# A hybrid decoder layer in split fp32: groups of 3, 4, 4 in the first FFN, earlier weight splits, later low halves, scaling from PSUM

## The chip, the cores and the metric

The kernel runs on one core of a Trainium2 chip. Its engines work from queues of their own, in order: TensorE (PE) multiplies, with its weight loads as PEld; VectorE (DVE), ScalarE (ACT) and GpSimd (POOL) do the elementwise work; DMAs are issued from SyncE (SP), ACT and POOL. The metric is the device time of one execution in microseconds.

## The reference

512 rows of 1024 columns get 16 learned rows ahead of them (528 rows), and pass one layer: half a SwiGLU FFN, a mixer (a gated short convolution beside forgetting attention), half a second FFN, a final norm.

```python
def swiglu_ffn(h, w_gu, w_down):
    gate, up = jnp.split(h @ w_gu, 2, axis=-1)
    return (jax.nn.silu(gate) * up) @ w_down
...
    h = jnp.concatenate([meta, x], axis=1)
    for l in range(DEPTH):
        h = h + 0.5 * swiglu_ffn(rms_norm(h, ffn1_norm[l]), ffn1_w_gu[l], ffn1_w_down[l])
        h = h + hybrid_mixer(rms_norm(h, mix_norm[l]), w_in[l], conv_w[l], b_f[l],
                             out_norm_conv[l], out_norm_attn[l], w_out[l])
        h = h + 0.5 * swiglu_ffn(rms_norm(h, ffn2_norm[l]), ffn2_w_gu[l], ffn2_w_down[l])
    h = h[:, N_META:]
    return rms_norm(h, final_norm)
```

The FFN's inner width is 2816, that is 22 tiles of 128 columns; a pair is two of them.

## The kernel before

Activations lie transposed (`hT`, 8 tiles of 128 rows of the model width by 528 columns). Every fp32 operand is split in a rounded high half, which ACT casts (hi), and a rest, which DVE takes by subtraction (lo). A product is then three matmuls, hi·hi, hi·lo and lo·hi.

Most of an FFN runs in units of a Strassen-like scheme (`products`). A unit takes a block of 256 output columns, cuts the rows in two halves (264 columns each in FFN1, 256 in FFN2) and makes seven products in place of eight, each in a slot of its own: nj pairs of k tiles, 3·nj matmuls. Slot b is the product of the weight form "nat" with B11; slot b + 1 is the last product (p4) of the unit before; then nat·B21, B·T2 with weight "s24", E·T1 with "s1", B·T3 with "s3" and C·B22. The PSUM banks A, B, C and E are reused within a unit: B starts as -A, copied by ACT at b + 1 (L535), and C as -B at b + 4 (L536), the latter beside the E product.

The weight forms come from `prep`: SP loads the raw block 15 slots ahead (L470), ACT copies one quarter (L474), POOL issues two accumulating DMAs (L478), DVE makes two adds (`s2` L481, `s4` L484), then ACT casts each form (L492) and DVE takes the low half (L496). The operand's forms of a pair come from `pair_forms`: sums on POOL (L379 to L382), casts on ACT (L368), low halves on DVE (L369). `x_pair` does so for the input, `hidden_pair` for the result of gate and up.

The first six column tiles of FFN1 and the first ones of FFN2 go the plain way (`classical`, `prep_classical`: load, cast L450, low half L454; 48 matmuls of L318 a tile), so that PE has work while forms are made. Then `gates` and `ups` of two tiles each alternate, with four pairs, and between them the `down` units, four for each group of hidden pairs: 3, 3, 2 and 3 in FFN1, and 3, 3 and 4 in FFN2. As the last group of FFN1 finishes a tile of `hT`, `operand` makes the mixer's operand from it: hi by ACT (L275), lo by DVE (L280), and `squares` adds on POOL (L290).

The order is written by hand: `sl.slot` appends a product, and `sl.at(t, work, prio)` sets the other engines' work at a slot number; each engine takes its work in the order of slots and, within one, of prio. At the end `finish(i)` norms the four row tiles of 128: squares and row sums on ACT, gain on DVE, the norm's few steps on ACT and DVE, scaling by it on ACT (L1230) and DVE (L1232), and one DMA for each half.

## Time and profile before

| | |
|---|---|
| median of three runs | 996.2 us (993.84 to 996.5) |
| profiled execution, its own time | 994.59 us |
| its span, first to last instruction | 992.6 us |
| PE, DVE, ACT, POOL busy | 96%, 79%, 59%, 35% |
| mean granted clock of PE | 0.989 |
| chain that ended last | PE 73%, DVE 15%, ACT 5% |

The span is 2.0 us shorter than the time. The chain's shares say which engine's work stood on the path that ended last, over the whole span; what a stretch is short of must be read from that stretch, from PE's idle time and from the clock that was granted there. A matmul that begins an idle time names in brackets how long PE stood and who ended it.

### The profile page before, as it was taken

Reading aid. Unit: us, or ns where it says so; the run is one execution under the profiler, and the core shown is the slowest. Engines: PE = TensorE matmul, PEld = TensorE weight load, DVE = VectorE, ACT = ScalarE, POOL = GpSimd, SP = SyncE. Lnnn points to the kernel's source line nnn. Section 1 sums busy time; section 2 is a strip of 40 time slices with the busy share of each in tenths; the row PEclk is TensorE's granted clock in tenths of the full one; section 3 lists DMA queues with packets and bytes.
Section 4 is the critical chain, followed back from the end, with each engine's and each line's share of the span. In section 5 each row is a group of like instructions: output and inputs, shape, how many; then the busy total and the mean of one; then the engine's idle time right before and its main releaser. Section 6 shows DMA issues by size and latency. Waiting matters only on the chain.

```text
span 992.6 us, 17859 instructions
## 1 busy us (share of the span) xinstructions
PE 948.9 (96%) x7022; PEld 905.7 (91%) x7022; DVE 780.0 (79%) x1260; ACT 583.3 (59%) x1036; POOL 345.6 (35%) x319
## 2 busy tenths in 40 slices
PE   9898999999999898999999999999999999999994
PEld 8798999999999887989899978778999999999993
DVE  5688887888788887786777666778887888788764
ACT  5545655665576564775656665446555665667444
POOL 4347533543444563100000000266443553354300
PEclk9999999999999999999999999999999999999998
DMA  6237488668784571532222221247778668787712
GB/s 194 65 107 145 118 174 159 148 120 181 171 151 97 117 142 32 144 103 60 74 66 78 57 84 43 64 137 151 138 157 190 132 133 181 146 180 149 174 29 86
DMA packets 173188, 121.01 MB, mean 122 GB/s; under 512 B 5844, under 2 KB 171520, under 8 KB 173104
## 3 DMA queue, kind: packets, MB, share of 16 engines
q1 hardware_dynamic: 113376, 89.37, 29.6%
q0 software_dynamic: 59008, 28.93, 23.9%
q10 hardware_dynamic: 720, 1.57, 0.4%
q8 instruction: 55, 0.90, 0.4%
q14 instruction: 29, 0.24, 0.1%
HBM read 117.69 MB, written 2.10 MB: 121 GB/s over the span
## 4 chain that ended last, share of the span: by engine, by line
PE 73%; DVE 15%; ACT 5%; issue 4%; DMA 1%; POOL 1%; SPq 0%; ACTq 0%; DVEq 0%
PE bank L522 47%; PE bank L318 20%; DVE w_lo L496 4%; DVE arena L369 2%; PE bank L1055 2%; DMA raw<-in_ffn_w_gu_dram 1%; DVE hT L604 1%; PE bank L1210 1%; DVE w_lo L454 1%; PE bank L992 1%; PE bank L1022 1%; ACT arena L275 1%; DVE w_lo L81 1%; DVE xn L398 1%; PE acc L318 1%
## 5 line engine op out<-in xcount | busy, mean ns | idle before, releaser
L522 PE MATMUL bank<-arena,w_hi 128*128 128x256 f32 (+1 forms) x3080 | 567.7, 286 | 13.3 <-ACT bank L536 7.7
L522 PEld LDWEIGHTS bank<-arena,w_hi 128*128 128x128 f32 x3080 | 481.7, 191 | 19.7 <-ACT bank L536 11.4
L522 PE MATMUL bank<-arena,w_lo 128*128 128x264 f32 (+1 forms) x1540 | 439.1, 285 | 4.2 <-DVE w_lo L496 4.2
L522 PEld LDWEIGHTS bank<-arena,w_lo 128*128 128x128 f32 x1540 | 294.6, 191 | 5.5 <-DVE w_lo L496 5.2
L492 ACT CAST w_hi<-raw 128x1024 fp32r<-128x1024 f32 (+2 forms) x186 | 176.3, 948 | 137.1 <-DVE raw L484 109.7
L318 PE MATMUL bank<-arena,w_hi 128*128 128x264 f32 (+2 forms) x1152 | 246.6, 322 | 2.6 <-ACT w_hi L450 2.6
L496 DVE TENSOR_TENSOR w_lo<-raw,w_hi 128x1024 fp32r<-128x1024 f32 (+2 forms) x186 | 222.9, 1199 | 25.8 <-ACT w_hi L492 24.2
L318 PEld LDWEIGHTS bank<-arena,w_hi 128*128 128x128 f32 x1152 | 178.9, 190 | 18.4 <-ACT w_hi L450 3.0
L318 PE MATMUL bank<-arena,w_lo 128*128 128x264 f32 (+2 forms) x576 | 155.0, 323 | 5.3 <-DVE w_lo L454 5.3
L318 PEld LDWEIGHTS bank<-arena,w_lo 128*128 128x128 f32 x576 | 96.2, 190 | 15.8 <-DVE w_lo L454 8.2
L478 POOL DMA_DIRECT2D raw<-in_ffn_w_gu_dram x34 | 44.1, 1297 | 82.2 <-DMA raw<-in_ffn_w_gu_dram 81.2
L478 POOL DMA_DIRECT2D s<-in_ffn_w_gu_dram x34 | 50.6, 1489 | 61.0 <-ACT bank L536 60.2
L80 ACT CAST w_hi<-raw 128x1024 fp32r<-128x1024 f32 (+3 forms) x54 | 44.1, 828 | 45.9 <-PE bank L318 36.0
L81 DVE TENSOR_TENSOR w_lo<-raw,w_hi 128x1024 fp32r<-128x1024 f32 (+2 forms) x53 | 55.3, 1052 | 18.0 <-ACT w_hi L80 17.7
L478 POOL DMA_DIRECT2D s<-in_ffn_w_down_dram x28 | 41.2, 1472 | 69.1 <-ACT bank L536 63.5
L604 DVE TENSOR_TENSOR hT<-bank,hT 128x264 f32<-128x264 f32 (+1 forms) x112 | 47.5, 424 | 14.9 <-PE bank L522 14.1
L496 DVE TENSOR_TENSOR w_lo<-s,w_hi 128x512 fp32r<-128x512 f32 (+2 forms) x62 | 46.8, 755 | 0.0
L193 ACT ACTIVATE s<-s 128x256 f32<-128x256 f32 (+3 forms) x42 | 19.3, 460 | 46.1 <-DVE s L561 26.7
L474 ACT COPY s<-raw 128x512 f32<-128x512 f32 (+2 forms) x62 | 35.5, 572 | 18.5 <-DVE w_lo L496 15.6
L481 DVE TENSOR_TENSOR raw<-raw 128x512 f32<-128x512 f32 (+2 forms) x62 | 41.4, 669 | 0.8
L369 DVE TENSOR_TENSOR arena<-ts,arena 128x1056 fp32r<-128x1056 f32 (+1 forms) x29 | 35.9, 1237 | 7.5 <-ACT arena L368 7.5
L478 POOL DMA_DIRECT2D raw<-in_ffn_w_down_dram x28 | 35.4, 1264 | 15.2 <-DMA raw<-in_ffn_w_down_dram 14.5
(229 smaller groups left out, 1158.0 us busy)
## 6 DMA issues: line engine op xcount, KB each, us to landing
raw<-in_ffn_w_gu_dram SPq DMA_DIRECT2D x34, 1024.0 KB, 7.0
raw<-in_ffn_w_down_dram SPq DMA_DIRECT2D x20, 768.0 KB, 4.4
raw<-in_w_in_dram SPq DMA_DIRECT2D x24, 512.0 KB, 4.0
raw<-in_ffn_w_gu_dram POOLq DMA_DIRECT2D x34, 256.0 KB, 4.7
s<-in_ffn_w_gu_dram POOLq DMA_DIRECT2D x34, 256.0 KB, 6.3
raw<-in_ffn_w_gu_dram SPq DMA_DIRECT2D x16, 512.0 KB, 4.0
raw<-in_ffn_w_down_dram SPq DMA_DIRECT2D x4, 1024.0 KB, 5.1
raw<-in_ffn_w_down_dram POOLq DMA_DIRECT2D x20, 192.0 KB, 4.4
```

The source lines that it names most:

```text
L80: nc.scalar.copy(h, src)
L81: nc.vector.tensor_sub(lw, src, h.bitcast(F32))
L318: nc.tensor.matmul(ap, lhsT=wt[:, kw, :], rhs=mt[:, k, c0 - off:c1 - off], start=(first and a == 0 and b == 0), stop=(last and a == len(ks ...
L369: self.sl.at(t + 1, lambda: nc.vector.tensor_sub(lo, src(), hi.bitcast(F32)), 2)
L474: nc.scalar.copy(raw["s3"], raw["all"][:, 0::2, 0])
L478: nc.gpsimd.dma_start(out=t, in_=mat_j[:, i, :, c0 + P:c0 + 2 * P], accum_op=ALU.add)
L481: nc.vector.tensor_add(raw["all"][:, 0::2, 0], raw["all"][:, 0::2, 1], raw["all"][:, 0::2, 0])
L492: nc.scalar.copy(w[nm_][0][:, :m], src(nm_))
L496: nc.vector.tensor_sub(w[nm_][1][:, :m], src(nm_), w[nm_][0][:, :m].bitcast(F32))
L522: nc.tensor.matmul(bank, lhsT=wt[:, idx(j), :], rhs=r[:, form, part], start=(start and i == 0), stop=(i == last), skip_group_check=True)
L604: return lambda: nc.vector.tensor_add(t, ps, t)
L1055: nc.tensor.matmul(oo, lhsT=lt, rhs=rt, start=(a == 0 and n_ == 0), stop=(a == 1 and n_ == len(ops) - 1))
```

## The change

- **Start.** The weights of tile f = 2 (gate and up) are loaded by SP before the row norm (`raw2`), the first cast on ACT comes ahead of `row_rstd`, the second behind the table load and the copy `out_of(a3)`. The transpose of the gains stands ahead of the product a3.
- **Classical weights** load, cast and subtract three slots earlier (`t - 11`, `t - 5`, `t - 4`), in both FFNs. The forms of hidden pair 0 start at slot 4 instead of 5.
- **`prep`**: copy and accumulating DMAs two slots later (`b - 9`, `b - 8`); in the first unit (no p4 yet) the two adds, "nat" and "s24" one slot earlier.
- **Groups** 3, 4, 4 in FFN1, so 12 down units instead of 16. `gates(14)` runs ahead of the second group and `ups(14)` behind it. The last group follows directly on the last `ups`; its last pair gets its forms from `last_pair`, with the sums on DVE, and its first unit takes its products in the order p6, p2, p5 (`late`).
- **Mixer operand**: the low half seven slots behind the high half. The mixer's first products take hi·hi and lo·hi for all eight k, then the forget gate's hi·hi, and only then what needs the low half.
- **FFN2's last weights** load and split some slots earlier.
- **`finish`**: for three of four row tiles DVE multiplies PSUM by norm and gain in one instruction, and both halves leave from SP's queue; the fourth stays as it was.

```diff
-    def operand(d, gcol, n, to, early=None):
+    def operand(d, gcol, n, to, early=None, part=None):
...
-            nc.scalar.activation(xh[:, d, o], hT[:, d, c], AF.Copy, scale=g)
+            if part != 1:
+                nc.scalar.activation(xh[:, d, o], hT[:, d, c], AF.Copy, scale=g)
+            if part == 0:
+                return
...
+        def last_pair(self, j, b):
...
+            def sums():
+                t = v["t"] = self.pool.tile([P, 4, h], F32, name="ts")
+                nc.vector.tensor_sub(t[:, 0], src(0, 0), src(0, 1))
+                nc.vector.tensor_add(t[:, 1], t[:, 0], src(1, 1))
+                nc.vector.tensor_sub(t[:, 2], src(0, 1), src(1, 1))
+
+            split(F_B11, 1, lambda: src(0, 0), b + 3)
+            split(F_B22, 1, lambda: src(1, 1), b + 6)
+            sl.at(b + 7, sums, 0)
+            split(F_T1, 3, lambda: v["t"][:, :3], b + 7)
+            sl.at(b + 9, lambda: nc.vector.tensor_sub(v["t"][:, 3], src(1, 0), v["t"][:, 1]), 0)
+            split(F_B21, 1, lambda: src(1, 0), b + 9)
+            split(F_T4, 1, lambda: v["t"][:, 3], b + 9)
...
-            self.sl.at(t - 8, load, 3)
-            self.sl.at(t - 2, hi, 3)
-            self.sl.at(t - 1, lambda: nc.vector.tensor_sub(w["w"][1], w["r"], w["w"][0].bitcast(F32)), 3)
+            self.sl.at(t - 11, load, 3)
+            self.sl.at(t - 5, hi, 3)
+            self.sl.at(t - 4, lambda: nc.vector.tensor_sub(w["w"][1], w["r"], w["w"][0].bitcast(F32)), 3)
...
-            sl.at(b - 11, base, 3)
-            sl.at(b - 10, add, 3)
-            sl.at(b - 2, s2, 3)
-            sl.at(b - 1, s4, 3)
-            for nm_, t in (("nat", b - 4), ("s24", b), ("s1", b + 1), ("s3", b + 2)):
+            sl.at(b - 9, base, 3)
+            sl.at(b - 8, add, 3)
+            c = b - 1 if self.p4 is None else b
+            sl.at(c - 2, s2, 3)
+            sl.at(c - 1, s4, 3)
+            for nm_, t in (("nat", c - 4), ("s24", c), ("s1", b + 1), ("s3", b + 2)):
...
+            for p in (p6, p2, p5) if late else (p2, p6, p5):
+                sl.slot(p)
...
+        raw2 = []
+        for c in (2 * P, DFF + 2 * P):
+            raw2.append(pool1.tile([P, 2048], F32, name="raw", bufs=3)[:, :1024].rearrange("p (k c) -> p k c", c=P))
+            nc.sync.dma_start(out=raw2[-1], in_=gu1.rearrange("(k p) n -> p k n", p=P)[:, :, c:c + P])
...
+            mm(a3, W.take(3), range(4, ND), xh, xl, first=False)
+            wts2 = [split_raw2(0)]
+            row_rstd(sa)
             table(SILU_SET)
+            out_of(a3)
+            wts2.append(split_raw2(1))
...
-        F.hidden_pair(0, 5, 5, True)
+        F.hidden_pair(0, 4, 4, True)
...
+        F.gates(14)
         for m in range(0, ND, 2):
-            F.down(3, 3, m)
-        g_units(range(14, NF))
+            F.down(3, 4, m)
+        t = F.ups(14)
+        F.hidden_pair(7, t, t)
+        g_units(range(16, NF - 2))
+        F.gates(NF - 2)
+        F.ups(NF - 2)
+        F.last_pair(NF // 2 - 1, len(sl.pe) - 7)
         for m in range(0, ND, 2):
-            F.down(6, 2, m)
-        for m in range(0, ND, 2):
-            for i, t in enumerate(F.down(8, 3, m)):
+            for i, t in enumerate(F.down(7, 4, m, m == 0)):
                 def fin(d=m + i):
-                    operand(d, GMIX, L, xm)
+                    operand(d, GMIX, L, xm, part=0)
                     squares(d, L, nc.gpsimd)
                 sl.at(t, fin, 1)
+                sl.at(t + 7, lambda d=m + i: operand(d, GMIX, L, xm, part=1), 1)
...
-        mm(acc_q, W.take(), range(ND), xh, xl)
...
+        for b, mt in enumerate((xh, xl)):
+            for p in (0, 2) if b == 0 else (1,):
+                mm(acc_q, W.take(), range(ND), xh, xl, only=p)
+            for k in range(ND):
...
-                sl.at(n - 10 + 6 * i, W.load, 4)
-                sl.at(n - 4 + 3 * i, lambda: W.split(False), 4)
+                sl.at(n - 22 + 7 * i, W.load, 4)
+                sl.at(n - 6 + 3 * i, lambda: W.split(False), 4)
...
-                    nc.vector.tensor_mul(zs[b], pss[i][b], gb[:, b * 512:(b + 1) * 512])
+                    if i == 3:
+                        nc.vector.tensor_mul(zs[b], pss[i][b], gs[b])
...
-                    if b == 0:
+                    if i < 3:
+                        stt(zs[b], pss[i][b], r, gs[b], ALU.mult, ALU.mult)
+                    elif b == 0:
```

ACT's queue at the start, from the second half of the row norm to the first cast of the weights of f = 2, before:

```order
L193 ACTIVATE y0_482<-sm_453,eps_74 128x264
L193 ACTIVATE y0_482<-y0_482 128x264
L185 ACT_TABLE_LOAD
L296 ACTIVATE tt_483<-y0_482 128x264
L718 COPY raw_494<-acc_427 128x528
L450 CAST w_hi_524<-raw_520 128x1024
```

and after, from the cast of the sums to the end of the norm's first half:

```order
L307 CAST arena_70<-ssum_69 128x528
L750 CAST w_hi_497<-raw_428 128x1024
L193 ACTIVATE y0_501<-sm_467,eps_74 128x264
L193 ACTIVATE y0_501<-y0_501 128x264
L299 ACTIVATE tt_502<-y0_501 128x264
```

The weights' cast stood last and now stands ahead of the whole norm.

DVE's queue in the middle of the last group of down units, where s2 and s4 of the next weight block, two results (L604) and the mixer operand's low half (L280) stand, with the engines waited for, before:

```order
L481 TENSOR_TENSOR raw_4135<-raw_4135 128x3x128 [waits DMASW2_49,DVE_49]
L604 TENSOR_TENSOR hT_67<-bank_516,hT_67 128x264 [waits DVE_49,PE_49]
L484 TENSOR_TENSOR raw_4135<-raw_4135 128x3x128 [waits DVE_49]
L604 TENSOR_TENSOR hT_67<-bank_518,hT_67 128x264 [waits PE_49]
L280 SCALAR_TENSOR_TENSOR arena_70<-hT_67,gains_75,arena_70 128x528 [waits Activation_49]
L496 TENSOR_TENSOR w_lo_4341<-raw_4135,w_hi_4340 128x768
```

and the same place after:

```order
L509 TENSOR_TENSOR raw_4040<-raw_4040 128x4x128 [waits DMASW4_49,DVE_49]
L635 TENSOR_TENSOR hT_67<-bank_530,hT_67 128x264 [waits DVE_49,PE_49]
L512 TENSOR_TENSOR raw_4040<-raw_4040 128x4x128 [waits DVE_49]
L635 TENSOR_TENSOR hT_67<-bank_532,hT_67 128x264 [waits PE_49]
L283 SCALAR_TENSOR_TENSOR arena_70<-hT_67,gains_75,arena_70 128x528
L524 TENSOR_TENSOR w_lo_4298<-raw_4040,w_hi_4297 128x1024 [waits Activation_49]
```

The low half at this place (L280, now L283) is that of a tile finished a unit earlier, and no longer waits for ACT; the weight's low half behind it waits for its own cast.

ACT's queue where the last group of down units begins, after (`s_3726` and `ts_3928` are the last hidden pair and its sums; `w_hi_3933` is "s24" of the first unit; L566 copies -A to B), with the engines waited for:

```order
L502 COPY s3_3890<-raw_3787 128x512 [waits DMAHW0_49,DVE_49,Activation_49]
L417 CAST arena_70<-s_3726 128x264 [waits DVE_49]
L417 CAST arena_70<-ts_3928 128x3x264 [waits DVE_49]
L520 CAST w_hi_3933<-raw_3660 128x1024 [waits PE_49]
L566 ACTIVATE bank_530<-bank_528 128x264 [waits PE_49]
```

Before, two-pair units stood at this place, and the casts of the last hidden pair (L368) came within the group ahead of the one that uses them; now the cast of the sums stands ahead of the weight cast and the bank copy of the very unit that uses them.

## Rows read from the trace of the kernel before

**Rows 1.** The page's first part: busy time, share of span, instructions of each engine

```profile
PE 948.9 (96%) x7022; PEld 905.7 (91%) x7022; DVE 780.0 (79%) x1260; ACT 583.3 (59%) x1036; POOL 345.6 (35%) x319
```

**Rows 2.** Stretches: width; busy PE, PEld, DVE, ACT, POOL (count); PEclk, DMA share, GB/s

```profile
40.44:92.02 51.58, 49.71 (x385) 48.66 (x385) 43.71 (x57) 22.23 (x31) 28.15 (x25) 0.97 0.47 121
92.02:99.00 6.98, 4.51 (x27) 4.29 (x26) 6.46 (x8) 3.65 (x6) 5.06 (x6) 0.79 0.60 72
328.00:350.00 22.00, 19.05 (x142) 17.52 (x142) 20.82 (x45) 12.88 (x27) 11.82 (x12) 1.00 0.70 147
360.00:394.00 34.00, 28.21 (x198) 26.32 (x197) 26.80 (x41) 18.02 (x33) 13.75 (x14) 0.95 0.22 33
636.90:683.00 46.10, 40.20 (x182) 32.43 (x181) 40.51 (x46) 23.14 (x34) 33.59 (x29) 0.96 0.51 126
```

**Rows 3.** PE in order of time, the start: start, duration, instruction, idle before, releaser

```profile
37.98 0.25 PE L721 MATMUL sm<-ident,gt 36*128 36x36 f32 x1
40.44 0.76 PE L318 MATMUL bank<-arena,w_hi 128*128 128x264 f32 x4 [2.20 <-ACT w_hi L450]
41.70 0.81 PE L318 MATMUL bank<-arena,w_lo 128*128 128x264 f32 x2 [0.51 <-DVE w_lo L454]
```

**Rows 4.** DVE and ACT in order of time, the start

```profile
36.89 0.43 DVE L298 SCALAR_TENSOR_TENSOR rs<-tt,y 128x264 f32<-128x264 f32 x1
...
39.34 1.05 ACT L450 CAST w_hi<-raw 128x1024 fp32r<-128x1024 f32 x1
```

**Rows 5.** PE in order of time, the first gates unit of FFN1

```profile
96.11 0.81 PE L522 MATMUL bank<-arena,w_hi 128*128 128x264 f32 x2 [2.47 <-ACT bank L535]
```

**Rows 6.** PE in order of time, first unit of the two-pair downs

```profile
330.40 0.51 PE L522 MATMUL bank<-arena,w_hi 128*128 128x264 f32 x2 [0.83 <-ACT bank L536]
...
330.87 0.40 PE L522 MATMUL bank<-arena,w_hi 128*128 128x264 f32 x2
...
332.33 0.41 PE L522 MATMUL bank<-arena,w_hi 128*128 128x264 f32 x2
```

**Rows 7.** PE's waits, 360 to 394 and 630 to 684: total, times, longest

```profile
PE bank L522 <- DVE w_lo L496: 4.2, 4, 1.8
PE bank L522 <- ACT bank L536: 1.6, 2, 1.2
...
PE bank L318 <- DVE w_lo L454: 3.8, 5, 1.5
PE bank L522 <- ACT bank L535: 2.1, 1, 2.1
```

**Rows 8.** DVE in order of time, second unit of the last downs of FFN1

```profile
370.89 0.77 DVE L280 SCALAR_TENSOR_TENSOR arena<-hT,gains,arena 128x528 fp32r<-128x528 f32 x1 [1.70 <-ACT arena L275]
371.58 2.09 DVE L496 TENSOR_TENSOR w_lo<-raw,w_hi 128x768 fp32r<-128x768 f32 x1
...
373.94 0.94 DVE L496 TENSOR_TENSOR w_lo<-raw,w_hi 128x768 fp32r<-128x768 f32 x1
```

**Rows 9.** PE, ACT and DVE in order of time, the finish

```profile
979.55 0.39 PE L1210 MATMUL bank<-w_lo,arena 128*128 128x512 f32 x1
...
979.96 0.60 ACT L1222 ACTIVATE sq<-bank 128x512 f32<-128x512 f32 x1 [0.41 <-PE bank L1210]
...
984.62 0.60 ACT L1222 ACTIVATE sq<-bank 128x512 f32<-128x512 f32 x1 [0.47 <-ACT zg L1230]
...
985.35 1.41 DVE L1224 TENSOR_TENSOR zg<-bank,ts 128x512 f32<-128x512 f32 x2 [1.43 <-ACT sq L1222]
```

**Rows 10.** Groups by line and shape (busy us, mean ns), and L478's transfers

```profile
L496 DVE TENSOR_TENSOR w_lo<-raw,w_hi 128x1024 fp32r<-128x1024 f32 x114 | 151.1, 1326 | 21.3 <-ACT w_hi L492 19.8
L492 ACT CAST w_hi<-raw 128x1024 fp32r<-128x1024 f32 x114 | 119.0, 1044 | 72.8 <-DVE raw L484 60.7 <-PE bank L522 12.1
L368 ACT CAST arena<-ts 128x1056 fp32r<-128x1056 f32 x15 | 16.0, 1067 | 6.1 <-POOL ts L382 6.1
...
DMA to landing us min/median/max: 3.5/4.9/9.3
```

More of the change, by code (lines that the diff above doesn't have):

```diff
@@ L506, in prep, with products @@
             return w
-        def products(self, nj, rhs, w):
+        def products(self, nj, rhs, w, late=False):
             sl, h = self.sl, self.h
@@ L704, in layer @@
                         squares(d + 1, L, nc.gpsimd)
-                for j in range(3):
-                    t = t528("raw")
-                    accs[j].each(lambda ps, g: nc.scalar.copy(g(t), ps))
-                    raws_f.append(t)
-                h, lo = split2(ssum, L)
-                a3, _ = new1()
-                mm(a3, W.take(3), range(4), xh, xl, last=False)
-                sms = [ps1s.tile([P, 512], F32, name="sm") for _ in range(2)]
-                sa = Acc(sms, L)
-                row_sums(sa, h, lo)
@@ L717, in layer, with split_raw2, out_of @@
+        with tc.manual_schedule(engines={mybir.EngineType.PE, mybir.EngineType.Activation, mybir.EngineType.DVE}):
+            def split_raw2(i):
+                w = (wts.tile([P, 8, P], F32R, name="w_hi"), wts.tile([P, 8, P], F32R, name="w_lo"))
+                nc.scalar.copy(w[0], raw2[i])
+                nc.vector.tensor_sub(w[1], raw2[i], w[0].bitcast(F32))
+                return w
+            def out_of(acc):
                 t = t528("raw")
-                a3.each(lambda ps, g: nc.scalar.copy(g(t), ps))
+                acc.each(lambda ps, g: nc.scalar.copy(g(t), ps))
@@ L735, in new @@
         return Acc([bank() for _ in range(1 if n <= 512 else 2)], n)
-    with tc.tile_pool(name="ffn1", bufs=1, reuse_waits="tile") as pool, tc.manual_schedule(engines=ENGINES):
+    with ffn1, tc.manual_schedule(engines=ENGINES):
+        pool = pool1
         sl = Slots()
```

59 lines of the change are left out of this document (35 added, 24 removed).

## Prediction

> **What bounds the kernel now.** I read the page's first part first. PE is busy 948.9 of 992.6 us, DVE 780.0, ACT 583.3 [rows 1], so only time in which PE stands still, or runs at half clock, can be won or lost; all matmuls of before stay (a product of nj pairs is 3 nj matmuls, and the groups still sum to 11 pairs). I therefore asked for busy time by stretch and, inside each, PE in order of time with what it waited for. [Rows 2] has the five stretches that matter. Idle is width minus PE busy; (1 - PEclk) times the width is what a clock at 1.2 instead of 2.4 GHz took besides. By this rule: classical units 1.9 + 1.5 = 3.4 us, first Strassen gates unit 2.5 + 1.5 = 3.9, downs with two pairs 2.95 + 0, last downs of FFN1 5.8 + 1.7 = 7.5, start of FFN2 5.9 + 1.8 = 7.7. Ahead of them PE stands 2.20 us for one weight cast [rows 3], and after PE's last matmul the finish runs 12.7 us [rows 9]. That is 25.5 us under PE and 2.2 before it; the other stretches lose little.
>
> **The change part by part.** 1) *Start.* PE waits at 40.44 for the cast L450, which ACT starts at 39.34 behind the table load and the second half of the row norm [rows 3, 4]. The change loads these weights (f = 2) earlier and casts them on ACT ahead of the row norm, where ACT idles; then PE is held by the norm's first half alone, done on DVE at 36.89 + 0.43 = 37.3, or by its own work up to 37.98 + 0.25 = 38.2. Gain 2.2 less a residue: 2.0 (1.0 to 2.3). The table load now follows the whole norm, 0.4 us later on ACT, and the second weight has 48 matmuls, 5.9 us, of cover.
>
> 2) *Classical weights and the first Strassen unit of FFN1.* Weight load, cast and low half move three slots (some 4.3 us) earlier; the pair forms of hidden pair 0 one slot earlier; in the first Strassen unit the two adds and the casts of "nat" and "s24" one slot earlier, because that unit has no p4 product between. This is aimed at the 0.51 us on L454 [rows 3] and the 2.47 us on L535 [rows 5], where ACT's bank copy stands in its queue behind a cast that waits for DVE. The losses to win are 3.4 + 3.9 = 7.3. The limit is DVE: 43.7 + 6.5 = 50.2 us of work in 58.6 us [rows 2]. Without the losses PE needs 51.3, so DVE would have to be 98% busy. I take 6.0 (3.0 to 7.3); zero would need DVE not to get ahead at all, and the idle it has now excludes that.
>
> 3) *Later POOL accumulates.* In all 58 Strassen units (after the change 16 + 12 in FFN1, 18 + 12 in FFN2) the copy L474 and the accumulating DMAs L478 come two slots later. They then have six slots to the add that reads them. A matmul takes 0.122 us (twelve from 330.87 to 332.33, [rows 6]), a slot of four pairs twelve of them: 6 x 12 x 0.122 = 8.8 us, with three pairs 6.6. From issue to landing the rows show 4.9 us as median and 9.3 at most [rows 10]. No wait on L481 or L484 for a DMA stands in the trace. So I cost it at nothing; what hides it is those six slots, and if that cover is gone DVE blocks in order, and behind it PE (the slower rival). By the nearest rows the bounds are 0 and (9.3 - 8.8) = 0.5 us a unit, 29 us in all. The Trainium skill, "SBUF — State Buffer", section "SBUF: two separate sides", speaks against this edit: GpSimd can't write the descriptors of a DMA issued from POOL while VectorE holds the port pair that they share, so it starts late when VectorE is busy. By the page's figures (a transfer of some 620 ns took some 3100 ns beside such a VectorE instruction), as an estimate, each would land 2.5 us later, and in the units with three pairs (12 of them) 0.8 us past six slots: by it the sum would be some 10 us less. The landing times of [rows 10] were taken beside a DVE that is 79% busy and hold whatever it does to them, so I go by them.
>
> 4) *Down groups 3, 4, 4 instead of 3, 3, 2, 3.* Four of 16 units go. With two pairs the E product that covers ACT's copy of bank B (L536) takes 6 x 0.122 = 0.73 us, and the copy comes late: 0.83 us idle at 330.40, and the first pair of matmuls behind it takes 0.51 instead of 0.40 [rows 6]. With four pairs the cover is 1.47 us. All 2.95 us of that stretch [rows 2] should go. Gain 2.9 (2.5 to 4.5, the upper end with the smaller waits of the second group of before).
>
> 5) *Last downs.* 7.5 us are lost. PE waits 4.2 us in all for the weights' low halves and 1.6 for L536 [rows 7], because DVE stands 1.70 us at the operand's low half L280 for ACT's L275, with the weight's L496 queued right behind [rows 8] (the same in two more units). The change issues those low halves seven slots later, when L275 is long done, so DVE doesn't wait there. L496 at 371.58 itself took 2.09 us, and one of the same size at 373.94 0.94 [rows 8]; that part may stay (1.15 us in a unit, under cover once the 1.70 us ahead of it are gone). The mixer's first products take all high halves first: eight hi-hi and eight lo-hi products of 264 columns come before any low half.
>
> A new cost stands in the same place. Before, the two-pair units ran between the last hidden product and the downs that use it. Now the last ups unit is followed by downs on its own pair, and the sums move to DVE. I followed that queue from the end of the ups' C product: two DVE steps of 264 columns, 0.43 us each as L298 [rows 4], the low half of B22 0.4 and three sums of 0.4 make 2.4; ACT's cast of T1 to T3 0.8 (three quarters of L368's 1.07), then in its queue the weight's cast 1.04 [rows 10] and the copy L535, some 0.4: PE may start B·T2 at about 4.6. Two products cover 2 x 12 x 0.122 = 2.93, so 1.7 us of wait. The weight's low half ends 1.33 us after the cast, at 5.5, and PE wants it at 4.85: 0.6 more. The clock may take 0.7: 3.0 us. The bounds are 1, with every step pipelined, and 8, with each as stretched as the L496 of 2.09. Net 7.5 - 3.0 = 4.5 (0 to 6.5).
>
> 6) *Start of FFN2.* The same edits as in 2. PE waits 3.8 us for L454 and 2.1 for L535 [rows 7]; 7.7 us with the clock. DVE is busy 40.5 of 46.1 us there [rows 2], so at most 5.6 us can go unless DVE's work leaves the stretch. 5.0 (2.5 to 7.7). The last weights of FFN2 load and split a little earlier, beside a busy PE: nothing.
>
> 7) *Finish.* Each of four finishes is a serial chain on ACT, 4.66 us from squares to squares (979.96 to 984.62) [rows 9]; of it, waiting for DVE's norm and the scaling L1230 go, since three of four are scaled on DVE straight from PSUM. ACT then needs some 2.9 us for each, and the last can start right behind PE at 980.0. But its two DVE products queue behind the two scalings of the third finish, 0.7 us each (1.41 for two from PSUM), and start 1 us late. Gain 4.66 - 1.0 = 3.7 (2.8 to 4.7).
>
> 8) *Restarts.* Behind each of about 20 waits that go, the first matmuls cost another 0.1 to 0.2 us (0.51 against 0.40 in [rows 6]): 3.0 (1 to 4).
>
> Sum: 2.0 + 6.0 + 0 + 2.9 + 4.5 + 5.0 + 3.7 + 3.0 = 27.1. The profiled run took 994.59 (span 992.6 and 2.0 outside it): 994.6 - 27.1 = 967.5. The runs of before have a median of 996.2, 1.6 above it, so I say 968.
>
> **The rivals.** *DVE sets the pace at both starts.* For: 50.2 us of work in 58.6, 40.5 in 46.1, and POOL's sums ahead of its low halves. Against: its idle time now lies in front of just those waits. Then half of parts 2 and 6 stays, 5.5 us: 973.5. *The new join costs 8 us*, when POOL's adds or the dropped clock stretch each step of the chain: 5 us more, 973. For: the 2.09 us [rows 8]. Against: the sums are on DVE now. *The change doesn't do what it says in the last downs:* the weights' low halves stay late for their own reasons, so that half of the 7.5 us stays: 972. *Slower:* the accumulates land after their add. The point from which this decides is a landing past 8.8 us (6.6 with three pairs). At the slowest seen it costs 0.5 us in each of 58 units, 29 us, and eats the whole gain; at 0.4 us later still 52 us, and the kernel is at 968 + 52 = 1020. Against: a median of 4.9.
>
> **How the numbers follow.** My forecast, about 968, gets 0.58; DVE's pace 0.20; the join 0.10; the last downs 0.06; a better sum with all upper ends 0.03; the late accumulates 0.03. The range holds the forecast and the first three rivals with their own scatter: 958 to 979; the ends of the unknown costs would by themselves reach past it only where several fall together. About 0.3% (3 us) is what a measurement of this kernel can tell from no change. All cases but the last are faster by more: faster 0.96, same 0.01, slower 0.03.
>
> **What would show it.** In the changed trace: PE's first bank matmul by 38.5 instead of 40.44; no wait over 0.5 us on the classical weights' low halves; no wait of 2 us on the bank copy in either first gates unit; DVE without idle time at the operand's low half; one new wait of PE of 1 to 3 us at the first down unit of the last group; the last finish's squares within 0.5 us of PE's end; waits of DVE's adds (L481, L484 of before) for a DMA in the short units would show the slower rival. I am wrong if PE's idle time in the two starts stays over 6 us in all, or if the join alone takes more than 5.

## The result, and the profile after

The changed kernel takes 973.0 us (median of four runs, 970.66 to 974.61) against 995.4: the ratio is 0.977, with a 95% interval of 0.975 to 0.980. I had said 968 within 958 to 979. The profiled execution took 974.61 with a span of 972.9, so 19.7 us of span went. The first part of its page, and its stretches in the form of [rows 2] (width; busy PE, PEld, DVE, ACT, POOL; clock; DMA):

```profile
PE 942.8 (97%) x7022; PEld 904.8 (93%) x7022; DVE 772.5 (79%) x1215; ACT 577.2 (59%) x1007; POOL 334.6 (34%) x307
```

```profile
40.00:86.99 46.99, 46.99 (x387) 46.99 (x385) 42.29 (x56) 22.71 (x32) 27.63 (x23) 1.00 0.44 119
86.99:104.56 17.57, 13.25 (x87) 13.04 (x85) 14.21 (x17) 11.15 (x19) 9.65 (x10) 0.81 0.38 76
613.10:658.67 45.57, 44.64 (x193) 35.79 (x192) 37.60 (x45) 23.43 (x33) 24.53 (x20) 1.00 0.44 131
658.67:676.50 17.83, 12.89 (x85) 12.18 (x84) 17.05 (x19) 10.42 (x17) 12.68 (x11) 0.81 0.68 112
```

The classical stretch of FFN1 now has no idle time of PE at all, where it had 1.9 us and a dropped clock [rows 2]. But the 17.6 us behind it, the first Strassen unit, hold 4.3 us of idle time and a clock of 0.81, and FFN2's first unit does the same. Over the same matmuls PE stands 10.2 us in the two starts (0.0 and 4.3 in FFN1, 0.9 and 4.9 in FFN2), where it stood 10.7 before (1.9 and 2.5, 4.3 and 2.1): its idle time there has moved and hardly shrunk. PE's waits there, and at the new join, in order of time:

```profile
92.93 0.81 PE L551 MATMUL bank<-arena,w_hi 128*128 128x264 f32 x2 [4.32 <-ACT bank L566]
...
334.17 0.51 PE L551 MATMUL bank<-arena,w_hi 128*128 128x264 f32 x2 [1.69 <-ACT bank L566]
335.15 0.39 PE L551 MATMUL bank<-arena,w_lo 128*128 128x264 f32 x1 [0.47 <-DVE w_lo L524]
...
661.38 0.39 PE L551 MATMUL bank<-arena,w_lo 128*128 128x256 f32 x1 [2.31 <-DVE w_lo L524]
665.25 0.80 PE L551 MATMUL bank<-arena,w_hi 128*128 128x256 f32 x2 [2.06 <-ACT bank L566]
```

The first answers to [rows 5]: the same wait on the same bank copy has grown from 2.47 to 4.32 us. The two at the join are the new ones. To see where the time went I cut both traces, and those of the experiments, at the same places of PE's queue: the first matmul to a bank, the first Strassen matmul, 84 matmuls later, and so on ("rows" are PE's matmuls behind FFN2's last Strassen unit). Microseconds of each piece:

| | to first bank matmul | FFN1 classical | first 84 Strassen matmuls | rest of FFN1 and mixer | FFN2, 192 classical and 84 Strassen matmuls | rest of FFN2 | rows | finish |
|---|---|---|---|---|---|---|---|---|
| before | 40.44 | 51.58 | 14.49 | 518.49 | 63.77 | 276.90 | 14.25 | 12.64 |
| changed | 40.00 | 46.99 | 17.57 | 508.52 | 63.42 | 274.14 | 14.45 | 7.81 |
| changed, second profile | 38.87 | 46.99 | 16.12 | 509.94 | 63.53 | 274.12 | 14.45 | 7.82 |
| classical back | 39.00 | 50.92 | 11.92 | 508.63 | 65.17 | 274.14 | 14.46 | 7.81 |
| copy back | 38.67 | 46.99 | 16.89 | 513.53 | 63.03 | 276.53 | 14.46 | 7.83 |
| low halves on ACT | 38.86 | 46.99 | 12.65 | 508.80 | 60.43 | 274.12 | 14.46 | 7.81 |
| accumulates late | 39.49 | 46.99 | 18.01 | 518.99 | 67.66 | 285.08 | 14.46 | 7.82 |
| join and finish | 39.03 | 46.98 | 16.34 | 508.33 | 62.84 | 274.13 | 14.46 | 6.89 |

Of the 19.7 us, 10.0 come from the rest of FFN1 with the mixer, 4.8 from the finish, 2.8 from the rest of FFN2, where I had costed everything at nothing, and only 1.5 + 0.35 from the two FFN starts, where I had looked for 11. The first piece and the third differ from profile to profile by 2 to 3 us with the same instructions (in the run of experiment 1, which alters only the finish, they are 39.61 and 14.33), so differences there count only where they are larger.

### The profile page after: what moved, and what is told of

The parts are those of the page before. It is cut to its first block, busy times and chain, and to the rows that moved or that the text cites. A ratio compares the mean times of both kernels' runs of the same rounds, so it can differ in the third digit from the quotient of the medians.

```text
span 972.9 us, 17717 instructions
## 1 busy us (share of the span) xinstructions
PE 942.8 (97%) x7022; PEld 904.8 (93%) x7022; DVE 772.5 (79%) x1215; ACT 577.2 (59%) x1007; POOL 334.6 (34%) x307
## 4 chain that ended last, share of the span: by engine, by line
PE 72%; DVE 13%; ACT 6%; issue 4%; POOL 3%; DMA 1%; SPq 0%; DVEq 0%; ACTq 0%; POOLq 0%
PE bank L551 53%; PE bank L321 13%; PE bank L1108 2%; DVE w_lo L81 1%; DVE arena L372 1%; DVE w_lo L524 1%; ACT arena L276 1%; PE bank L1263 1%; PE bank L1075 1%; POOL ts L382 1%; PE acc L321 1%; PE bank L1045 1%; DVE w_lo L482 1%; POOL ts L381 1%; DVE arena L283 1%
## 5 line engine op out<-in xcount | busy, mean ns | idle before, releaser
L520 ACT CAST w_hi<-raw 128x1024 fp32r<-128x1024 f32 (+1 forms) x174 | 174.1, 1000 | 123.5 <-DVE raw L512 94.0
L524 DVE TENSOR_TENSOR w_lo<-raw,w_hi 128x1024 fp32r<-128x1024 f32 (+1 forms) x174 | 219.7, 1263 | 26.5 <-ACT w_hi L520 24.7
L321 PE MATMUL bank<-arena,w_lo 128*128 128x264 f32 (+2 forms) x576 | 152.1, 320 | 0.5 <-DVE w_lo L482 0.5
L506 POOL DMA_DIRECT2D s<-in_ffn_w_gu_dram x34 | 45.0, 1324 | 109.0 <-ACT s L502 108.7
L81 DVE TENSOR_TENSOR w_lo<-raw,w_hi 128x1024 fp32r<-128x1024 f32 (+2 forms) x53 | 55.0, 1051 | 15.2 <-ACT w_hi L80 14.8
L506 POOL DMA_DIRECT2D s<-in_ffn_w_down_dram x24 | 33.1, 1379 | 88.1 <-ACT s L502 88.1
L635 DVE TENSOR_TENSOR hT<-bank,hT 128x264 f32<-128x264 f32 (+1 forms) x96 | 40.6, 423 | 15.6 <-PE bank L551 13.9
L371 ACT CAST arena<-ts 128x1056 fp32r<-128x1056 f32 (+1 forms) x28 | 29.5, 1055 | 29.3 <-POOL ts L384 29.3
L524 DVE TENSOR_TENSOR w_lo<-s,w_hi 128x512 fp32r<-128x512 f32 (+1 forms) x58 | 45.2, 780 | 0.0
L509 DVE TENSOR_TENSOR raw<-raw 128x512 f32<-128x512 f32 (+1 forms) x58 | 39.6, 682 | 0.7
L512 DVE TENSOR_TENSOR raw<-raw 128x512 f32<-128x512 f32 (+1 forms) x58 | 38.9, 672 | 0.1
```

What stands on the lines that cost most here:

```text
L81: nc.vector.tensor_sub(lw, src, h.bitcast(F32))
L321: nc.tensor.matmul(ap, lhsT=wt[:, kw, :], rhs=mt[:, k, c0 - off:c1 - off], start=(first and a == 0 and b == 0), stop=(last and a == len(ks ...
L371: self.sl.at(t, lambda: nc.scalar.copy(hi, src()), 2)
L506: nc.gpsimd.dma_start(out=t, in_=mat_j[:, i, :, c0 + P:c0 + 2 * P], accum_op=ALU.add)
L509: nc.vector.tensor_add(raw["all"][:, 0::2, 0], raw["all"][:, 0::2, 1], raw["all"][:, 0::2, 0])
L512: nc.vector.tensor_add(raw["all"][:, 1::2, 0], raw["all"][:, 0::2, 0], raw["all"][:, 1::2, 0])
```

## The experiments

Each kernel is the changed one with one thing altered. Ratios are to the kernel before; the changed kernel, timed beside experiments 5 to 8, has 0.977 (0.975 to 0.980) there too. The kernel before had medians of 997.1, 995.2 and 997.5 us beside experiments 1 to 4, 5 to 8 and 9 to 12, so a difference of 2 us between kernels of two of these groups isn't told by medians alone.

### 1. The finish of before

```diff
-                    if i == 3:
-                        nc.vector.tensor_mul(zs[b], pss[i][b], gs[b])
+                    nc.vector.tensor_mul(zs[b], pss[i][b], gs[b])
...
-                    if i < 3:
-                        stt(zs[b], pss[i][b], r, gs[b], ALU.mult, ALU.mult)
-                    elif b == 0:
+                    if b == 0:
...
-                    (nc.scalar if i == 3 and b == 0 else nc.sync).dma_start(out=out[i * P:(i + 1) * P, b * 512:(b + 1) * 512], in_=zs[b])
+                    (nc.scalar, nc.sync)[b].dma_start(out=out[i * P:(i + 1) * P, b * 512:(b + 1) * 512], in_=zs[b])
```

> The changed kernel with the finish of before (gain on DVE first, then scaling by the norm on ACT and DVE, in all four row tiles); all else as changed. Theory (ACT's chain of four finishes): from PE's end to the span's end 12.6 instead of 7.8 us, so the time is 4.9 us over the changed kernel's 973.0: 978. Rival (the shorter finish is the DMA's doing, since both halves now leave from one queue): the last DMA is the same in both, so under 2 us: 974 to 975.

Measured: 977.2 us, ratio 0.979 (0.976 to 0.982). From PE's end to the span's end it takes 12.4 us instead of 7.8, so the finish is worth 4.6 us; by the medians 3.8 to 4.2. ACT's chain, as the theory says: the squares of the last two finishes stand 4.67 us apart again (961.19 and 965.86), as in [rows 9]. The edit puts the DMAs' queues back too, so it is this distance, and not the edit alone, that speaks against a part of theirs.

### 2. Classical weights at the old slots

```diff
-            self.sl.at(t - 11, load, 3)
-            self.sl.at(t - 5, hi, 3)
+            self.sl.at(t - 8, load, 3)
+            self.sl.at(t - 2, hi, 3)
```

(and the low half at `t - 1`)

> The changed kernel with the classical weights' load, cast and low half at the slots of before (8, 2 and 1 ahead instead of 11, 5 and 4), in both FFNs. Theory (the gain of the classical stretch is mostly handed on to the first Strassen unit, which waits for the chain of pair forms POOL sums, ACT cast, DVE low half): PE loses some 2 to 3 us in FFN1's classical stretch again, and its wait of 4.3 us at the first bank copy shrinks by as much, likewise in FFN2: the time within 2 us of 973. Rival (the two losses are independent): 3 to 4 us in FFN1 and 4 in FFN2 come back whole: 980.

Measured: 973.9 us, ratio 0.976 (0.973 to 0.979), the same as the changed kernel. PE's waits in FFN1 from the first bank matmul to behind the first Strassen unit (engine, line, what it waited for: total, times, longest):

```profile
PE bank L321 <- DVE w_lo L482: 1.8, 4, 0.7
PE bank L321 <- ACT w_hi L478: 1.0, 1, 1.0
PE bank L551 <- DVE w_lo L524: 0.7, 1, 0.7
PE bank L551 <- ACT bank L566: 0.5, 1, 0.5
```

4.0 us in seven small waits, or in the changed kernel 4.3 us in one: the earlier weights took the waits out of the classical stretch and handed them on. In the table the classical piece is 3.9 us longer and the Strassen piece 4 to 6 shorter. In FFN2 the old slots cost 1.7 us net.

### 3. Copy and accumulates at the old slots

```diff
-            sl.at(b - 9, base, 3)
-            sl.at(b - 8, add, 3)
+            sl.at(b - 11, base, 3)
+            sl.at(b - 10, add, 3)
```

> The changed kernel with copy and accumulating DMAs of every weight block 11 and 10 slots ahead again instead of 9 and 8. Theory (they are hidden at either place; the pair forms set the pace at both starts): the time within 1.5 us of 973, the waits of 4.3 us (FFN1) and 2.3 + 2.1 us (FFN2) stay. Rival (the accumulates, moved later, stand in POOL's queue ahead of the last pair's sums and hold them up): these waits shrink by 2 us each, 969.

Measured: 979.5 us, ratio 0.982 (0.979 to 0.986): 5 us slower by the ratios, 6 by the medians, against both expectations. The first units' waits stayed (4.3 us in FFN1), but 2.4 to 3.8 us came in the rest of FFN1 and mixer (against the two profiles of the changed kernel) and 2.4 in the rest of FFN2, with 11 waits of up to 0.7 us, 4.3 us in all, on the second bank copy, of which the changed kernel has none. So the edit that I had costed at nothing is one of the larger gains. Experiment 9 says why.

### 4. Low halves of the mixer's operand at once

```diff
-                    operand(d, GMIX, L, xm, part=0)
+                    operand(d, GMIX, L, xm)
                     squares(d, L, nc.gpsimd)
                 sl.at(t, fin, 1)
-                sl.at(t + 7, lambda d=m + i: operand(d, GMIX, L, xm, part=1), 1)
```

> The changed kernel with the mixer operand's low half straight behind its high half again (groups 3, 4, 4 and the mixer's new order stay). Theory: DVE stands 1.6 us at each low half for ACT in the units of the last group, and the weight's low half behind it comes late: PE waits 1 to 1.7 us in three of four units, with some half clock: 4 to 6 us, 977 to 979. Rival (with four pairs a unit lasts 10.3 us instead of 7.7, so that the wait is covered): under 1.5 us, 973 to 974.5.

Measured: 975.5 us, ratio 0.978 (0.975 to 0.981). By time it is within the scatter of the changed kernel. By the trace the rest of FFN1 is 4.3 us longer (PE waits for low halves 0.86, 1.03, 0.84 and 1.02 us), and the mixer 1.3 us shorter, since PE comes later to a wait that stands there now (1.7 us at the scores, for the casts of the keys). Both were partly right: the waits come back, each at 1 us rather than 1.7, and something behind takes a part. The edit is worth some 1 to 3 us.

### 5. The changed kernel again

> The changed kernel itself, beside the runs of this chip, as the measure for the others. Both theories: 972 to 975, the wait ahead of the first bank copy of FFN1 anywhere between 2.3 and 4.3 us, since it was 4.3 in its first profile and 2.3 in that of the run with the finish put back, whose instructions up to there are the same.

Measured: 973.4 us (971.85 to 973.55), ratio 0.977 (0.975 to 0.980). The first bank copy made PE wait 4.30 us.

### 6. First Strassen unit's adds earlier

```diff
-            sl.at(c - 2, s2, 3)
-            sl.at(c - 1, s4, 3)
+            e = b - 5 if self.p4 is None else b - 2
+            sl.at(e, s2, 3)
+            sl.at(e + 1, s4, 3)
```

(copy and accumulates of that unit at b - 11 and b - 10.) In this kernel the weights "nat" of that one unit are cast behind the add that overwrites them, so that product takes other numbers; the work is the same.

> The changed kernel with the two adds of the first Strassen unit's weights five and four slots ahead (three and two in the changed kernel), and their copy and accumulating DMAs eleven and ten ahead, so that DVE does them before the low half of the last pair's sums, for which it stands some 3 us. Theory (the order in DVE's queue makes the wait: the adds, ACT's cast and its bank copy are queued behind a low half that waits for POOL's sums): the waits of 2.3 to 4.3 us (FFN1) and 2.3 + 2.1 (FFN2) shrink to under 1.5 each, 4 to 7 us in all with the clock: 967 to 969. Rival (DVE has more work in the two starts than time, 50 of 52 us and 40 of 41): the waits only go to other instructions of the same stretches: 972 to 974.

Measured: 972.8 us, ratio 0.977 (0.974 to 0.979). The 4.3 us on the bank copy became 1.5 on it and 2.5 on two low halves; in FFN2 the 2.3 + 2.1 became 3.3 + 1.8 + 0.5. The waits only went to other instructions, so the order in DVE's queue isn't what makes them; the rival's outcome came. For FFN2 the run says less: there DVE's first add stood 2.85 us for its accumulating DMA (657.50), a cost that the edit brought with it.

### 7. The join

```diff
-            c = b - 1 if self.p4 is None else b
+            c = b - 1 if self.p4 is None or late else b
...
-            split(F_T1, 3, lambda: v["t"][:, :3], b + 7)
+            for f in (F_T2, F_T1, F_T3):
+                split(f, 1, lambda f=f: v["t"][:, f - F_T1], b + 8, 1)
```

> The changed kernel with another order at the join of the last ups unit and the last downs: the weight 's24' of that unit is added and cast one slot earlier, the bank copy stands ahead of the casts of the sums, and T2, which is used first, gets its high and low half first. Theory (the 1.7 + 0.5 us of wait there are ACT's queue: cast of three sums, weight cast, bank copy in series): the waits of PE there fall to under 1.2 us in all, and the time by 1.0 to 2.0 us: 971 to 972. Rival (the sums themselves are late, DVE ends them only some 2.4 us after the ups' C product): the waits stay within 0.5 us, 973.

Measured: 972.9 us, ratio 0.976 (0.973 to 0.980). PE's wait on the bank copy at the join is gone, but it waits 0.73 and 0.70 us for weights' low halves instead of 1.69 and 0.47. The waits are 0.7 us shorter, the rest of FFN1 with the mixer takes 508.1 us, against 508.5 and 509.9: half of the theory at most, and too little to time.

### 8. The old groups

The groups 3, 3, 2, 3 and the order of before, with the later copies and low halves:

```diff
-            F.down(3, 4, m)
...
-        F.last_pair(NF // 2 - 1, len(sl.pe) - 7)
+            F.down(3, 3, m)
+        g_units(range(14, NF))
         for m in range(0, ND, 2):
-            for i, t in enumerate(F.down(7, 4, m, m == 0)):
+            F.down(6, 2, m)
+        for m in range(0, ND, 2):
+            for i, t in enumerate(F.down(8, 3, m)):
```

> The changed kernel with the down groups of before (3, 3, 2, 3: 16 units, POOL sums for the last pair, first unit's products in the old order), with the later accumulates and the later low halves kept. Theory A (as predicted: the two-pair units have too little cover for ACT's copy, whatever else): the 3 to 4 us at the two-pair units come back, the join's 2.5 us go: 973.5 to 975. Theory B (those waits came from the early copy of the weight block in ACT's queue, which waits for a buffer that DVE frees; the run with the copy put back lost 3.7 us in FFN1's units with four and three pairs too): with the later copy two-pair units lose under 1.5 us, and without the join the time is 970.5 to 972.

Measured: 975.8 us (970.92 to 976.88), ratio 0.978 (0.975 to 0.982). Unclear by time. By the trace the rest of FFN1 with the mixer takes 510.6 us, 2.1 and 0.7 us longer than in the two profiles of the changed kernel, so the new join gives back a good part of what the groups save. The 168 matmuls of the two-pair units take 23.8 us, some 3 more than at 0.122 us each and as much as theory A wants, but not by its cause: the second bank copy (L567, before L536), on which PE waited 2.3 us in these units of the kernel before, isn't waited for there at all. PE's waits in them, from the first matmul of the units (321.36) on, are

```profile
328.04 0.51 PE L551 MATMUL bank<-arena,w_hi 128*128 128x264 f32 x2 [1.26 <-DVE hT L635]
329.36 0.51 PE L551 MATMUL bank<-arena,w_hi 128*128 128x264 f32 x2 [0.32 <-ACT bank L566]
335.39 0.51 PE L551 MATMUL bank<-arena,w_hi 128*128 128x264 f32 x2 [0.26 <-ACT bank L566]
```

and DVE is busy 22.4 of the 23.8 us. So theory B is right on the waits that the prediction was built on, though not on the size (under 1.5 us) nor the time; that what short units still lose comes of a DVE without time to spare is argued from its busy time and not shown.

### 9. Only the copy at the old slot

```diff
-            sl.at(b - 9, base, 3)
+            sl.at(b - 11, base, 3)
```

> The changed kernel with only ACT's copy of each weight block 11 slots ahead again; the accumulating DMAs stay 8 ahead. Theory (the gain of the later accumulates is that of the copy: at 11 ahead it stands in ACT's queue right ahead of the second bank copy of the unit that runs then, and it waits there for the buffer that DVE frees with the low half of 's3'): everything that the run with copy and DMAs put back lost is lost again, 4 to 6 us, 977.5 to 979.5. Rival (the accumulating DMAs were the cause, by POOL's queue or by traffic): within 1.5 us of the changed kernel's 973.4.

Measured: 978.5 us, ratio 0.982 (0.979 to 0.985): the whole loss of experiment 3, with the accumulates where the change puts them. ACT at the second gates and ups units, DVE beside it, and PE (columns as in [rows 4]):

```profile
108.37 0.51 ACT L502 COPY s<-raw 128x384 f32<-128x384 f32 x1 [1.56 <-DVE w_lo L524]
108.79 0.37 ACT L567 ACTIVATE bank<-bank 128x264 f32<-128x264 f32 x1
...
107.66 0.68 DVE L524 TENSOR_TENSOR w_lo<-s,w_hi 128x512 fp32r<-128x512 f32 x1
...
109.21 0.51 PE L551 MATMUL bank<-arena,w_hi 128*128 128x264 f32 x2 [0.65 <-ACT bank L567]
```

The copy L502 waits 1.56 us for DVE to free one of the two buffers "s3" with its low half (107.66 + 0.68 = 108.34), the bank copy L567 stands right behind it, and PE waits 0.65 us for that. Two slots later the copy stands behind the bank copy. The whole trace says the same: here ACT stands ahead of the copy 13 times for DVE's low half, and PE 11 times for the second bank copy, to the tenth as in experiment 3; in the kernel before, ACT stands ahead of this copy (L474) 23 times, 15.6 us in all, and in the changed kernel three times, 0.9. Here, before, and in the changed kernel:

```profile
  DVE w_lo L524: 10.0, 13
PE bank L551 <- ACT bank L567: 4.3, 11, 0.7
```

```profile
ACT s L474 <- DVE w_lo L496: 15.6, 23, 1.6
```

```profile
  DVE w_lo L524: 0.9, 3
```

The theory holds; a part of the accumulating DMAs isn't seen, as the run with them put back too (979.5) is 1 us away.

### 10. Four low halves on ACT

```diff
-            self.sl.at(t + 1, lambda: nc.vector.tensor_sub(lo, src(), hi.bitcast(F32)), 2)
+            if full:
+                self.sl.at(t + 1, lambda: nc.vector.tensor_sub(lo, src(), hi.bitcast(F32)), 2)
+            else:
+                self.sl.at(t, lambda: nc.scalar.copy(lo, src()), 2)
```

> The changed kernel in which the low halves of the input pairs' four sums aren't taken: ACT copies the sums to their place instead, so this part of the computation is changed. It takes 1.2 us from DVE for each of four pairs in either start and gives 1.1 us to ACT; POOL's sums and the buffer that they share stay. Theory (DVE's work is the limit of both starts): the waits at the first Strassen units, 4.3 us in FFN1 and 5.0 in FFN2, fall by 2 to 4 us each, and with the clock the time by 4 to 8: 966 to 969. Rival (POOL's sums, one pair after the other through one buffer, are the limit): the waits shrink by under 1 us each, 971.5 to 973.

Measured: 967.0 us, ratio 0.970 (0.967 to 0.973), 6.4 us below the changed kernel. PE's waits from the first bank matmul of FFN1 to behind the first Strassen unit:

```profile
PE bank L554 <- DVE w_lo L527: 1.4, 1, 1.4
PE bank L554 <- ACT bank L569: 0.5, 1, 0.5
```

1.9 us instead of 4.3; in FFN2 4.6 us instead of 5.0. The granted clock is 1.00 in both first units, where the changed kernel has 0.81, and that is most of the 3 us by which FFN2's piece is shorter. By the time and by FFN1's waits the theory has it; FFN2's waits fell by 0.4 us, as the rival had said. And the run changes more than DVE's work: DVE no longer stands behind POOL's sums for the low half of the last ones, and in FFN1 the last pair's four sums, the same instructions, took 4.1 us here and 6.5 in the changed kernel. So it shows what taking four low halves from DVE at each start is worth, and not that DVE's work alone sets the limit. Experiment 1's trace, whose instructions are the changed kernel's up to its finish, shows the sums' part. Two of the last pair's sums on POOL, and PE's wait:

```profile
79.86 1.68 POOL L381 TENSOR_TENSOR ts<-xn 128x264 f32<-128x264 f32 x1
81.62 0.82 POOL L382 TENSOR_TENSOR ts<-ts,xn 128x264 f32<-128x264 f32 x1
...
90.51 0.52 PE L551 MATMUL bank<-arena,w_hi 128*128 128x264 f32 x2 [2.29 <-ACT bank L566]
```

All four took 4.5 us there instead of 6.5, and PE's wait is 2.29 us instead of 4.32, though DVE was busier in the classical stretch (44.6 us against 42.3). So POOL's sums have a part in FFN1's wait beside DVE's work; how large each part is no run separates.

### 11. Accumulates three slots ahead

```diff
-            sl.at(b - 9, base, 3)
-            sl.at(b - 8, add, 3)
+            sl.at(b - 6, base, 3)
+            sl.at(b - 5, add, 3)
```

> The changed kernel with copy and accumulating DMAs 6 and 5 slots ahead of their unit instead of 9 and 8, so that the transfers have three slots to the add, 4.4 us with four pairs and 3.3 with three, where 4.9 is the median of a landing. Theory (the slower rival has its point at the landing): DVE waits for the accumulates in most units by 0.5 to 2.5 us, and as its other work is queued behind, PE loses 0.3 to 1 us in each of 58 units: 985 to 1030. Rival (the queue in front of the add is so far behind its slot that the transfer has landed by then): under 3 us, 973 to 976.

Measured: 1001.0 us, ratio 1.003 (1.002 to 1.005): 27.6 us above the changed kernel, which is all that the change gains and 3 to 5 us more, since it is a little slower than the kernel before. From issue to landing, first here, then in the changed kernel (minimum, median, maximum):

```profile
DMA to landing us min/median/max: 3.9/7.7/10.5
```

```profile
DMA to landing us min/median/max: 3.9/4.8/9.0
```

And PE's and DVE's waits of the whole run:

```profile
PE bank L551 <- ACT bank L566: 27.5, 19, 6.5
...
DVE raw L509 <- DMA raw<-in_ffn_w_gu_dram: 8.8, 3, 4.0
```

PE stands for the bank copy 27.5 us in 19 waits, where the changed kernel has 9.0 in six, the longest in the two first units (6.1 and 6.5 us). DVE's adds now wait for an accumulating DMA, in three units (the theory had said most), which they never do in the changed kernel. That is at most a third of the loss. Another part is DVE's work itself, on the same number of instructions; its low halves of "s" first here, then in the changed kernel:

```profile
L524 DVE TENSOR_TENSOR w_lo<-s,w_hi 128x512 fp32r<-128x512 f32 x46 | 48.4, 1052 | 0.0
```

```profile
L524 DVE TENSOR_TENSOR w_lo<-s,w_hi 128x512 fp32r<-128x512 f32 x46 | 38.0, 826 | 0.0
```

DVE is busy 14.7 us longer in all (787.2 against 772.5). So issuing late has the price of the slower rival, and the point lies between eight slots and five; but waits for a landing are 8.8 us beside a loss of 27.6, and with the rest goes a DVE that is slowed, which I hadn't named. How the two act on each other no run separates.

### 12. The join, and the last finish's mean first

The edit of experiment 7, and:

```diff
-                    if i == 3:
-                        nc.vector.tensor_mul(zs[b], pss[i][b], gs[b])
                 m, y0, t, r = (t4[:, j:j + 1] for j in range(4))
                 nc.vector.tensor_scalar(m, sums[:, 0:1], sums[:, 1:2], 1.0 / D, ALU.add, ALU.mult)
+                for b in range(2 if i == 3 else 0):
+                    nc.vector.tensor_mul(zs[b], pss[i][b], gs[b])
```

> The changed kernel with the join's other order (as in the run on the join) and, in the last finish, the mean of squares on DVE ahead of the two products with the gain instead of behind them. Theory (in the last finish DVE holds ACT up by 1.27 us with these products): from PE's end to the span's end 7.0 instead of 7.8 us, the join 0.5 us less, so 1.3 us in all: 972. Rival (the DMA's landing sets the end, whatever is ahead of it): 972.9.

Measured: 969.9 us (968.76 to 971.0), ratio 0.973 (0.970 to 0.975). The finish takes 6.9 us instead of 7.8: ACT waits 0.39 us for the mean (L1279) and no longer 1.59 (L1280 of the changed kernel).

```profile
967.47 0.29 ACT L193 ACTIVATE t<-t,eps 128x1 f32<-128x1 f32 x1 [1.59 <-DVE t L1280]
```

```profile
963.27 0.29 ACT L193 ACTIVATE t<-t,eps 128x1 f32<-128x1 f32 x1 [0.39 <-DVE t L1279]
```

0.9 us of the finish and up to 0.7 of waits at the join are seen; the median is 3.5 us below that of experiment 5, and its interval overlaps the changed kernel's. This is the fastest complete kernel of the study by its median; the traces account for 1 to 1.5 us of it.

## Why the prediction was right, and where not

The time came 5 us above my number and well inside the range, the sign was sure, but several steps behind it were mis-sized and two had the wrong reason. My own sign of being wrong came true: PE's idle time in the two starts was to fall to 6 us or less, and it went from 10.7 to 10.2; both first units still wait over 2 us for the bank copy (4.32 and 2.06). The first rival, with 0.20, describes the starts better than my sum, though it too left them 5.5 us where 1.9 came, and its 973.5 us is nearer to the 973.0 measured. That my number came near all the same is luck, as the end of this section shows.

- **Start (2.0 us).** 0.4 us in the first profile, 0.3 to 2.2 in the thirteen of the changed kernel and its variants (38.26 to 40.17 against 40.44). In the four with least of it the granted clock was half for some 3 us behind 30 us, which the kernel before doesn't have there. The mechanism was right: PE has no wait at the first bank matmul any more; the size depends on the clock and, among the nine without the half clock (38.26 to 39.39), on something that no run isolates.
- **FFN1 classical and first unit (6.0 us).** This step failed: 1.5 us in the first profile, 3.0 in the second, 4.8 at best (experiment 1's). The classical piece gained 4.6 us, and the first unit's wait grew by 1.9 with more half clock. I had written that DVE would have to be 98% busy and took most of it anyway. Experiments 2 and 6 show that a wait taken away at one place of this stretch comes back at another, and 10 that it shrinks when DVE has less to do, as the rival says; but POOL's sums have a part in it too. In this trace DVE is idle for 3.17 us even there, since the low half of the last pair's sums is next in its queue and POOL's sums are slow (POOL at 80.27 and 83.00):

```profile
80.27 2.64 POOL L381 TENSOR_TENSOR ts<-xn 128x264 f32<-128x264 f32 x1
83.00 2.33 POOL L382 TENSOR_TENSOR ts<-ts,xn 128x264 f32<-128x264 f32 x1
...
87.89 1.26 DVE L372 TENSOR_TENSOR arena<-ts,arena 128x1056 fp32r<-128x1056 f32 x1 [3.17 <-ACT arena L371]
```

  Experiment 6 put other work in that gap, and PE's waits stayed 4.0 us in all; in experiment 1's profile the gap is gone without any edit there, since the sums were faster, and the wait is 2.3.
- **FFN2's start (5.0 us).** The same failure: 0.2 to 0.9 us in the profiles that leave this piece alone (62.84 to 63.55 against 63.77). The bound of 5.6 us that I drew from DVE's idle time assumed that every idle microsecond could be filled; but DVE's idle time stood behind POOL's sums, and stayed there.
- **Later copies (0).** The step that failed with the other sign. I weighed the accumulating DMAs and gave bounds of 0 and a loss, without a reason to exclude a gain; ACT's copy moves along with them, past the bank copy L536 in ACT's queue. It is worth 5 us (experiments 3 and 9). The waits on L536 that [rows 6] show I had put down to short cover alone, where experiment 8 has the short cover and none of these waits, and the row "ACT s L474 <- DVE w_lo L496: 15.6, 23" stood in the waits of before.
- **Groups (2.9) and join (-3.0).** The join came out as worked out: 1.69 + 0.47 us of wait against 1.7 + 0.6, without the 0.7 of clock, as the clock held. The groups are worth 0.7 to 2.1 us net of the join by the trace, unclear by time. Their reason was wrong: of the 2.95 us of [rows 2] the 2.3 on L536 go with the later copy, and DVE, busy 20.82 of the 22.00 us in the same row, was what I should have read there.
- **Low halves (7.5 with the weights' low halves).** By experiment 4 the edit itself is worth 1 to 3 us; the larger part of the 7.5 went with something else, of which the later copies are one candidate (1.6 of it were waits on L536). Two waits for weights' low halves stay in the last downs (0.82 and 0.77 us), and 1.7 us of a new one stand in the mixer, ahead of the scores, of which I had said nothing. The piece as a whole gave 10.0 us against 7.4 for parts 4 and 5 and some of the 3.0 for restarts.
- **Finish (3.7).** 4.8 us. The last finish waits 0.7 us for the two scalings ahead of it (1.59 against 0.88 before) and not 1.0, the first of its two squares now runs ahead of PE's end (964.11, where PE ends at 965.10) and not behind it, and the last DMA ended 0.2 us sooner after its issue.
- **Restarts (3.0).** No run isolates them. In the rest of FFN1 with the mixer PE's idle time fell by 5.1 us (from 12.6 to 7.5), and 3.4 us at half clock took 1.7 before, where the first profile of the changed kernel has none; of the 10.0 us this leaves some 3, an estimate, for matmuls that were slower behind a wait.
- **Slower rival.** It didn't decide, since six slots to the add keep clear of it: no add waits for a DMA. With three the loss is 27.6 us for 58 units, 0.48 each, close to the 0.5 that I had given, but a third of it only by the waits that I had named. The Trainium skill, "SBUF — State Buffer", section "SBUF: two separate sides", would have had the kernel 10 us worse by my estimate; at the new slots the landing median is 4.8 us, as before, so that cost didn't appear. With still later slots it grew to 7.7, which that rule would allow, but no run tells it from other causes. My bound of 29 us was itself too low: it took 0.5 us for all 58 units, and by the same rows the 12 with three pairs would lose 9.3 - 6.6 = 2.7 each.

In the first profile 10.8 us are missing at the three starts (1.6, 4.5 and 4.7), and 6.5 came that I hadn't foreseen (2.8 in the rest of FFN2, 2.6 in FFN1 and mixer, 1.1 in the finish); that they offset is why the total was close. Taken back one at a time, the edits cost by the medians some 4 us (finish), 6 (copy), 2 (low halves), 2 to 3 (groups) and under 1 (classical weights), 15 to 16 of the 22 us; the start, the mixer's new order and the earlier adds were not taken back alone, so the rest isn't divided.

## What to carry to other kernels

When a step is moved in a table of slots, list what it now stands ahead of and behind on every engine that it uses: a copy of half a microsecond, waiting for a buffer, cost 5 us because bank copies were queued behind it. Where one engine is some 90% busy in a stretch (DVE 42.3 of 47.0 us here), a wait that is removed early in the stretch can come back at its end; take work from that engine instead, as the run that took four low halves from DVE at each start did (6.4 us). Add up PE's idle time over the whole stretch before and after, not wait by wait. An engine's idle time in such a stretch is slack only if nothing in its queue waits for another chain.

## What was not expected of the hardware

Thirteen profiles of the changed kernel and its variants run the same instructions up to the first bank matmul, and the same matmul behind 26 us (the 177th) starts within 2.2 us in them (26.7 to 28.9). In four of them (the first one and experiments 1, 8 and 11) the granted clock then was 0.5 for some 3 us, behind idle time that the others have as well; in those the first bank matmul started at 39.5 to 40.2 us, in the other nine at 38.3 to 39.4. So a gain of 1 us at a start can't be read from one profile. A POOL addition of 264 columns took 2.64 and 2.33 us (80.27 and 83.00 in the rows above) while DVE was busy, and 0.75 twice right behind (85.29 and 86.00), in DVE's gap of 3.17 us. In experiment 1's profile the same four took 1.68, 0.82, 1.22 and 0.75 us, and there DVE's instructions beside them were the longer ones: two low halves of 264 columns took 2.17 us (80.83) instead of 1.04, and a weight's 1.80 (83.60) instead of 1.21. Which of the two engines is held up differs between executions of the same instructions, and PE's wait behind them with it (2.29 or 4.3 us). And the transfers that accumulate took 7.7 instead of 4.8 us to land when they were issued three slots later; the cause stays open.
